# Paired 64-row gate matmuls, one attention block per pair of heads, and element-wise work on GpSimd in a two-layer hybrid step

## The chip, the core and the metric

The kernel runs on one core of a Trainium2 chip. A core has five engines with instruction queues of their own, each worked off in order: TensorE (PE, matrix products into PSUM banks), VectorE (DVE), ScalarE (ACT), GpSimd (POOL) and SyncE (SP, which here only issues DMAs). They wait for one another through semaphores. The metric is the device time of one execution in microseconds (us). The kernel before takes 1232.82 us, the median of three runs (1231.01 to 1233.5).

## What is computed

Two layers are applied to 128 context tokens and 256 latent tokens (384 columns here, features on the 128 partitions). Per layer, cut to what the change touches:

```
h = RMSNorm(x) * (1 + scale1) + shift1            # shift/scale/gate = SiLU(cond) @ w_mod + b_mod
u = h @ w_in                                      # u_pool, u_q, u_k, u_v, u_x, u_y, u_g (gates)
y_a = multi-scale pooling of u_pool, a 128x128 map per group
y_b = attention (context: dense; latent: neighbourhood + all context keys)
xc  = depthwise conv (width 4) of u_x
rg, ig = sigmoid(xc @ wa[block] + ba), sigmoid(xc @ wx[block] + bx)   # 2 directions, 8 blocks of 64 channels
h_t = a_t h_(t-1) + sqrt(1 - a_t^2) * ig_t * xc_t,  a = exp(c * rg * log_sigmoid(lambda))
y_c = (forward + backward h) * gelu(u_y)
merged = sum over the 3 branches of sigmoid(u_g) * (branch @ w_branch);  x += gate1 * (merged @ w_out)
x += gate2 * SwiGLU(...);  at the end a final RMSNorm
```

## The kernel before

**Matrix products.** A product is done in three passes to keep precision: weights and activations are each split into a high and a low part (`whi`/`wlo`, `hh`/`hl`, ...), and `mm3` (L342 to L344) multiplies high by high, high by low weight, low by high weight. A job of eight weight tiles is 24 matmuls of 384 columns; `in` jobs (a 1024x128 slice of w_in) have eight tiles, `br` jobs (w_branch) and `pw` (pooling map) four. Each weight tile is loaded by SP (`raw`), cast to `whi` by ACT (L305) and turned into `wlo` by DVE (L314), some jobs ahead, in the fixed order of `chunk_order()`.

**Order of work.** The code is a recording: every helper appends instructions to its engines' queues in program order, so what stands earlier in the code stands earlier in each queue. `job()` records a job's matmuls, then calls `tick()` (advances every open evacuation generator by one `yield`, and starts one of the waiting ones in `lazy`), `side_step()` (advances the side branches: the LRU scans and the attention), records its own evacuation, and calls `after(units)`. `after` adds `modr * units` to an accumulator `macc`, and for each whole unit records one `mod_step()`: half a row of SiLU(cond) @ w_mod, done on DVE as a product of a 128x1024 weight tile `wm` with `crow` (L262, output `junk`). `modr` is taken from the table `MR`, by layer and stage; its entry 6 holds for the five `in` jobs at the start of layer 0 (0.1 each there), entry 0 for the first stage of gate and branch jobs (`bi` = 0). The very first `mod_step()` calls `silu_crow()`: two tanh on ACT into `crt` (L233) and two updates of `crow` on DVE (L234). The tiles `crt` and `wm` share two buffers, so the load of the first `wm` (SP, L247) can't be issued before the first `crow` update has read its `crt`.

**A layer.** `in` jobs for the pool, x and y columns, with the pooling (`branch_pool`: `ws`, `pd`, split into `pdh`/`pdl`) and the convolution (`branch_conv`: `xp`, `cv`, split into `xch`/`xcl`) as evacuations; then `pool_proj` (four products of four groups: 12 matmuls, evacuated into `yah`, `yal`); then, for the branch order b = 0, 2, 1, eight pairs of a gate job (`win(24 + b*8 + d)`, evacuated by a tanh into `tg`) and a `br` job. During b = 0 the four `lru_gates(c)` stand at d = 2, 4, 6 and at the end; then the values job, the q/k jobs, b = 2 beside the attention, b = 1, and w_out. In layer 0 the pooling and convolution evacuations wait in `lazy`, since their inputs need a correction (`shw`, from the matmuls `mt`, L1168) that is computed at the end of `start()`, ahead of the five `in` jobs.

**Recurrent gates.** Each 64x64 block pair of wa and wx is stored as a block-diagonal 128x128 tile. `lru_gates(c)` does for each of the two directions two `mm3` of 386 columns over the full height, into two PSUM banks, and two tanh of 128 partitions (L616, L617).

**Attention.** 16 units (head pair p, query tile, head). A generator `branch_attn` does one step i per side step, in which the stages of the softmax of successive units are staggered: scores (64-row matmuls, both heads alternating, L702) at i, `soft_a` at i-1, `soft_b` at i-2, `soft_c` at i-3, transposes (full-height matmuls, L744) at i-4, their evacuation at i-5, values (64-column matmuls, L779) on every second step.

Of the kernel before, what the change touches and what calls it, by code (L numbers as in the profile page):

```python
# [90 lines left out]
def emit(ctx, tc, A, outs):  # L91
# [204 lines left out]
    def w_hi(n):  # L296
        while ws["cv"] < min(n, len(order)):
# [7 lines left out]
            S.activation(hi[:, :nk], r[:, :nk], AF.Copy)  # L305
# [298 lines left out]
    def lru_gates(l, c, w, y):  # L604
# [3 lines left out]
        for e in range(2):  # L608
            pa, px = psum(), psum()
            mm3(pa, w, (c % 2) * 4 + e * 2, mv, True, True, n=LW)  # L610
            mm3(px, w, (c % 2) * 4 + e * 2 + 1, mv, True, True, n=LW)

            def ev(pa, px, i, e):
# [13 lines left out]
                S.activation(t2[:, n], t2[:, n], AF.Identity, scale=-1.0, bias=1.0)  # L627
                y["lru", c, e] = (t2, th, ti)
            push(ev(pa, px, e * 4 + c, e))

    def branch_lru_scan(l, y):
# [13 lines left out]
        for c in range(4):  # L645
# [16 lines left out]
            V.tensor_tensor(yc[:, :NT], yc[:, :NT], hs[1][:, :NT], op=OP.add)  # L662
            V.tensor_tensor(yc[:, :NT], yc[:, :NT], y.pop(("gy", c))[:, :NT], op=OP.mult)
# [26 lines left out]

    def branch_attn(l, y):
# [90 lines left out]
        i = 0  # L782
        while i < nu + 7 or pend:
            if i < nu and ("k", units[i][0]) not in y:
                yield
# [4 lines left out]
            if 0 <= i - 1 < nu:  # L790
                p, hh, qt = units[i - 1]
                pr[i - 1] = soft_a(pr[i - 1], 2 * p + hh, qt)
            if 0 <= i - 2 < nu:
                soft_b(pr[i - 2])
            if 0 <= i - 3 < nu:
                soft_c(pr[i - 3])
# [81 lines left out]
    def ev_branch(th, bi, d, mg, mo):  # L878
        def f(ps):
# [55 lines left out]
    def start(y):  # L935
# [230 lines left out]
        ps = psum("mt")  # L1166
        for g in range(7):
            T.matmul(ps[:, 2 * g:2 * g + 2], sb[g // 3][:, (g % 3) * 128:(g % 3) * 128 + 128], sel,  # L1168
                     start=True, stop=True)
        shw = cp.tile([128, 14], F32, name="shw0")  # L1170
        V.tensor_copy(shw, ps[:, 0:14])
        evs = [ev_pool(0, g, y) for g in range(4)] + [ev_ux(0, c, y) for c in range(3)]
        for g, ev in enumerate(evs):
            lazy.append(ev((un[g], shw[:, 2 * g:2 * g + 2])))
# [137 lines left out]
def layout(i):  # L1312
# [37 lines left out]
    lru = np.zeros((L, 4, 2, 2, 128, 128), np.float32)  # L1350
    for w, name in enumerate(("lru_wa", "lru_wx")):
        a = f[name]
        for ch in range(4):
            for half in range(2):
                r = slice(64 * half, 64 * half + 64)
                lru[:, ch, :, w, r, r] = a[:, :, 2 * ch + half]
    A["lru"] = c(lru.reshape(L, 2, 8, 128, 128).transpose(0, 1, 3, 2, 4))
# [32 lines left out]
```

## Time and profile before

| what | value |
|---|---|
| median of 3 runs | 1232.82 us |
| profiled execution, its own time | 1231.6 us |
| its span (first to last instruction) | 1229.8 us |
| PE busy | 1219.8 us, 99% |
| DVE, ACT, POOL busy | 888.3 (72%), 598.4 (49%), 72.6 us (6%) |

The profile lists instructions with a start and a duration. A matmul's duration (0.33 us for 384 columns) overlaps its neighbour's: what one costs PE is the distance from its start to the next start. A group "x3" in a timeline is three like instructions in a row, from the first start to the last end. In brackets stands the idle time of the engine ahead of it and what ended that.

### The profile page before, as it was taken

Reading aid. Unit: us, or ns where it says so; the run is one execution under the profiler, and the core shown is the slowest. Engines: PE = TensorE matmul, PEld = TensorE weight load, DVE = VectorE, ACT = ScalarE, POOL = GpSimd, SP = SyncE. Lnnn points to the kernel's source line nnn. Section 1 sums busy time; section 2 is a strip of 40 time slices with the busy share of each in tenths; the row PEclk is TensorE's granted clock in tenths of the full one; section 3 lists DMA queues with packets and bytes.
Section 4 is the critical chain, followed back from the end, with each engine's and each line's share of the span. In section 5 each row is a group of like instructions: output and inputs, shape, how many; then the busy total and the mean of one; then the engine's idle time right before and its main releaser. Section 6 shows DMA issues by size and latency. Waiting matters only on the chain.

```text
span 1229.8 us, 19387 instructions
## 1 busy us (share of the span) xinstructions
PE 1219.8 (99%) x7348; PEld 1190.6 (97%) x7348; DVE 888.3 (72%) x1650; ACT 598.4 (49%) x1103; POOL 72.6 (6%) x187
## 2 busy tenths in 40 slices
PE   9999999999999999999999999999999999999997
PEld 7799999899999999999999999999999999999997
DVE  6798698998978887757779668787676785442432
ACT  5587845544455333333357576564344743332321
POOL 0000150000200000010000013100010000000000
PEclk9999999999999999999999999999999999999999
DMA  9635684466626666645643457632553355333321
GB/s 346 256 132 190 187 177 134 147 209 217 202 98 207 235 226 212 202 150 182 214 138 113 158 167 190 142 118 100 172 197 129 119 207 171 131 109 108 115 88 52
DMA packets 63645, 204.30 MB, mean 166 GB/s; under 512 B 7744, under 2 KB 10944, under 8 KB 63424
## 3 DMA queue, kind: packets, MB, share of 16 engines
q1 hardware_dynamic: 60912, 197.56, 48.2%
q0 software_dynamic: 2496, 5.25, 3.5%
q8 instruction: 57, 0.93, 0.3%
q14 instruction: 36, 0.29, 0.1%
q10 hardware_dynamic: 144, 0.26, 0.1%
HBM read 200.41 MB, written 2.63 MB: 165 GB/s over the span
## 4 chain that ended last, share of the span: by engine, by line
PE 58%; issue 22%; DVE 1%; POOL 0%; POOLq 0%; DVEq 0%
PE ps L342 18%; PE ps L344 18%; PE ps L343 18%; PE tp L744 1%; PE o L779 1%; PE sc L702 1%; PE vt L1210 0%; PE vt L1211 0%; PE vt L1212 0%; DVE junk L262 0%; DVE wlo L314 0%; PE o L774 0%; DVE pr L718 0%; PE st L473 0%; DVE yo L1306 0%
## 5 line engine op out<-in xcount | busy, mean ns | idle before, releaser
L342 PE MATMUL ps<-hh,whi 128*128 128x384 f32 x1256 | 422.2, 336 | 0.0
L344 PE MATMUL ps<-hl,whi 128*128 128x384 f32 x1256 | 419.9, 334 | 0.0
L343 PE MATMUL ps<-hh,wlo 128*128 128x384 f32 x1256 | 419.7, 334 | 0.0
L314 DVE TENSOR_TENSOR wlo<-raw,whi 128x1024 fp32r<-128x1024 f32 (+2 forms) x296 | 322.8, 1115 | 21.7 <-ACT whi L305 21.7
L305 ACT ACTIVATE whi<-raw 128x1024 fp32r<-128x1024 f32 (+2 forms) x296 | 279.8, 970 | 97.3 <-PE ps L344 59.8
L342 PEld LDWEIGHTS ps<-hh,whi 128*128 128x128 f32 x1256 | 235.7, 188 | 2.4 <-issue 0.3
L343 PEld LDWEIGHTS ps<-hh,wlo 128*128 128x128 f32 x1256 | 235.8, 188 | 0.1
L344 PEld LDWEIGHTS ps<-hl,whi 128*128 128x128 f32 x1256 | 235.7, 188 | 0.0
L262 DVE SCALAR_TENSOR_TENSOR junk<-wm,crow 128x1024 bf16<-128x1024 f32 x160 | 195.4, 1221 | 27.0 <-DMA wm<-in_wm 25.0
L909 ACT ACTIVATE ft<-ps 128x384 f32<-128x384 f32 x40 | 19.7, 493 | 202.8 <-PE ps L344 202.8
L342 PE MATMUL ps<-svh,whi 128*128 128x384 f32 x352 | 117.6, 334 | 0.0
L343 PE MATMUL ps<-svh,wlo 128*128 128x384 f32 x352 | 117.6, 334 | 0.0
L344 PE MATMUL ps<-svl,whi 128*128 128x384 f32 x352 | 117.6, 334 | 0.0
L894 DVE SCALAR_TENSOR_TENSOR x<-ps,modv,x 128x128 f32<-128x128 f32 x64 | 23.7, 412 | 81.6 <-PE ps L344 81.5
L911 DVE TENSOR_TENSOR ft<-ft,ps 128x384 f32<-128x384 f32 x40 | 22.1, 552 | 80.7 <-ACT ft L909 80.7
L872 ACT ACTIVATE tg<-ps 128x384 f32<-128x384 f32 x48 | 23.4, 489 | 89.0 <-PE ps L344 88.2
L342 PEld LDWEIGHTS ps<-svh,whi 128*128 128x128 f32 x352 | 66.1, 188 | 0.0
L343 PEld LDWEIGHTS ps<-svh,wlo 128*128 128x128 f32 x352 | 66.1, 188 | 0.0
L344 PEld LDWEIGHTS ps<-svl,whi 128*128 128x128 f32 x352 | 66.1, 188 | 0.0
L881 DVE SCALAR_TENSOR_TENSOR tg<-tg,ps 128x384 f32<-128x384 f32 x48 | 26.4, 551 | 44.0 <-PE ps L344 43.9
L453 ACT ACTIVATE sq<-x 128x384 f32<-128x384 f32 x40 | 20.1, 513 | 66.4 <-DVE x L894 66.4
L342 PE MATMUL ps<-mgh,whi 128*128 128x384 f32 x128 | 42.8, 334 | 0.0
(242 smaller groups left out, 1770.7 us busy)
## 6 DMA issues: line engine op xcount, KB each, us to landing
raw<-in_fi SPq DMA_DIRECT2D x88, 512.0 KB, 4.3
raw<-in_in SPq DMA_DIRECT2D x82, 512.0 KB, 3.9
wm<-in_wm SPq DMA_DIRECT2D x80, 512.0 KB, 4.3
raw<-in_fo SPq DMA_DIRECT2D x32, 512.0 KB, 4.6
raw<-in_br SPq DMA_DIRECT2D x48, 256.0 KB, 2.7
w<-in_wm SPq DMA_DIRECT2D x16, 512.0 KB, 7.0
raw<-in_wo SPq DMA_DIRECT2D x16, 512.0 KB, 3.7
raw<-in_fo SPq DMA_DIRECT2D x16, 384.0 KB, 3.1
```

The lines of the kernel that those rows point to most:

```text
L262: V.scalar_tensor_tensor(j, t, 0.5, crow[:, s], op0=OP.mult, op1=OP.mult, accum_out=modv[l][:, comp, d, s:s + 1])
L305: S.activation(hi[:, :nk], r[:, :nk], AF.Copy)
L314: V.tensor_tensor(lo[:, :nk], r[:, :nk], hi[:, :nk].bitcast(F32), op=OP.subtract)
L342: T.matmul(ps[:, :n], hi[:, k], mv[0][:, :n], start=start, stop=False)
L343: T.matmul(ps[:, :n], lo[:, k], mv[0][:, :n], start=False, stop=False)
L344: T.matmul(ps[:, :n], hi[:, k], mv[1][:, :n], start=False, stop=stop)
L453: S.activation(sq[:, :NT], xt[d], AF.Square)
L872: S.activation(t[:, :NT], ps[:, :NT], AF.Tanh, scale=0.5)
L881: V.scalar_tensor_tensor(t[:, :NT], t[:, :NT], 1.0, ps[:, :NT], op0=OP.add, op1=OP.mult)
L894: V.scalar_tensor_tensor(xt[d][:, o:o + n], ps[:, o:o + n], modv[l][:, comp, d, s:s + 1], xt[d][:, o:o + n], op0=OP.mult, op1=OP.add)
L909: S.activation(t[:, :NT], pg[:, :NT], AF.Silu)
L911: V.tensor_tensor(t[:, :NT], t[:, :NT], pu[:, :NT], op=OP.mult)
```

## The change

The recurrent gates are stored as 64x128 weights (wa for one half of the rows, wx for the other columns): `lru_gates` now records three pairs of matmuls per direction that use rows 0 to 63 and rows 64 to 127 into two banks, and evacuates with four tanh of 64 partitions. The four calls stand at d = 0, 2, 4, 6 in place of d = 2, 4, 6 and the end, so that the first follows `pool_proj` directly; `pool_proj`, with the emptying of `lazy` ahead of it, comes after the first gate job and not before it. In layer 0 the matmuls `mt` and what hangs on them (`rest()`) stand behind the first of the five `in` jobs. `MR` for layer 0 has 1.1 in place of 0.7 for the first stage, and 1.9, 1.6, 0.5 in place of 2.3, 1.8, 0.3 for the next three. The attention does transposes of two units, values and the next scores in one block on every second step. GpSimd takes the casts of the first branch's `br` weights and of the `vw` weights (from ACT), the affine step on `t2` (from ACT), the mask, the two steps on `yc` and the merge sums `mg` (from DVE); ACT takes the copy `ptc` from DVE. The diff, cut to its core:

```diff
-MR = ((0.7, 2.3, 1.8, 0.3, 1.3, 1.1, 0.1), (0.6, 0.8, 0.8, 0.3, 1.3, 0.7, 0))
+MR = ((1.1, 1.9, 1.6, 0.5, 1.3, 1.1, 0.1), (0.6, 0.8, 0.8, 0.3, 1.3, 0.7, 0))
...
-            S.activation(hi[:, :nk], r[:, :nk], AF.Copy)
+
+            if order[i][0] == "vw" or order[i][0] == "br" and order[i][2] < 8:
+                G.tensor_copy(hi[:, :nk], r[:, :nk])
+            else:
+                S.activation(hi[:, :nk], r[:, :nk], AF.Copy)
...
-            pa, px = psum(), psum()
-            mm3(pa, w, (c % 2) * 4 + e * 2, mv, True, True, n=LW)
-            mm3(px, w, (c % 2) * 4 + e * 2 + 1, mv, True, True, n=LW)
+            pb = [psum(), psum()]
+            j = (c % 2) * 2 + e
+            for wi, mi in ((0, 0), (1, 0), (0, 1)):
+                for b in range(2):
+                    r = slice(64 * b, 64 * b + 64)
+                    T.matmul(pb[b][:, :LW], w[wi][r, j], mv[mi][r, :LW], start=wi + mi == 0, stop=mi == 1)
...
-                S.activation(th[:, n], pa[:, n], AF.Tanh, scale=0.5, bias=q[:, i:i + 1])
-                S.activation(ti[:, n], px[:, n], AF.Tanh, scale=0.5, bias=q[:, 8 + i:9 + i])
+                for t, o, f in ((th, 0, 0), (ti, 8, 1)):
+                    for b in range(2):
+                        r, rs = slice(64 * b, 64 * b + 64), slice(64 * (b ^ f), 64 * (b ^ f) + 64)
+                        S.activation(t[r, n], pb[b][rs, n], AF.Tanh, scale=0.5, bias=q[r, o + i:o + i + 1])
...
-                S.activation(t2[:, n], t2[:, n], AF.Identity, scale=-1.0, bias=1.0)
+                G.tensor_scalar(t2[:, n], t2[:, n], -1.0, 1.0, op0=OP.mult, op1=OP.add)
...
-            V.tensor_tensor(yc[:, :NT], yc[:, :NT], hs[1][:, :NT], op=OP.add)
-            V.tensor_tensor(yc[:, :NT], yc[:, :NT], y.pop(("gy", c))[:, :NT], op=OP.mult)
+            G.tensor_tensor(yc[:, :NT], yc[:, :NT], hs[1][:, :NT], op=OP.add)
+            G.tensor_tensor(yc[:, :NT], yc[:, :NT], y.pop(("gy", c))[:, :NT], op=OP.mult)
...
-            V.tensor_tensor(t, t, cmask.unsqueeze(1).to_broadcast([128, 6, 64]), op=OP.add)
+            G.tensor_tensor(t, t, cmask.unsqueeze(1).to_broadcast([128, 6, 64]), op=OP.add)
...
-                V.tensor_copy(pc[:, :128], tp[:, 384:512])
+                S.activation(pc[:, :128], tp[:, 384:512], AF.Copy)
...
-            if 0 <= i - 5 < nu:
-                pr[i - 5] = evac(*pr[i - 5])
-            if i % 2 and 0 <= i - 7 < nu:
-                values((i - 7) // 2)
-            if 0 <= i - 4 < nu:
-                pr[i - 4] = transp(pr[i - 4])
-            if i % 2 == 0 and i < nu:
-                p, hh, qt = units[i]
-                if qt == 0:
-                    begin(p)
-                pr[i], pr[i + 1] = scores(p, qt)
+            if i % 2 == 0:
+                for u in (i - 6, i - 5):
+                    if 0 <= u < nu:
+                        pr[u] = evac(*pr[u])
+            else:
+                for u in (i - 5, i - 4):
+                    if 0 <= u < nu:
+                        pr[u] = transp(pr[u])
+                if 0 <= i - 7 < nu:
+                    values((i - 7) // 2)
+                if i + 1 < nu:
+                    p, hh, qt = units[i + 1]
+                    if qt == 0:
+                        begin(p)
+                    pr[i + 1], pr[i + 2] = scores(p, qt)
...
-            V.tensor_tensor(mg[d][:, :NT], mg[d][:, :NT], t[:, :NT], op=OP.add)
+            G.tensor_tensor(mg[d][:, :NT], mg[d][:, :NT], t[:, :NT], op=OP.add)
...
         for m in todo:
+            if m == 20 and l == 0:
+                rest()
...
-        while lazy:
-            tick()
-        tick()
-        pool_proj(l, y)
...
             win(24 + b * 8, ev_gate(th), units=0.67)
+            if b == 0:
+                while lazy:
+                    tick()
+                tick()
+                pool_proj(l, y)
             for d in range(8):
-                if b == 0 and d in (2, 6):
-                    lw = w_get("lru", l, d // 4)
-                if b == 0 and d in (2, 4, 6):
-                    lru_gates(l, d // 2 - 1, lw, y)
+                if b == 0 and d % 2 == 0:
+                    if d % 4 == 0:
+                        lw = w_get("lru", l, d // 4)
+                    lru_gates(l, d // 2, lw, y)
```

On DVE around the first `pool_proj` of layer 0 the queue stood like this before (`pdl` goes to `pool_proj`, `xcl` to the first recurrent gates, `crow` and `junk` belong to the first `mod_step`):

```order
L362 TENSOR_TENSOR pdl<-pd,pdh 128x384
L599 SCALAR_TENSOR_TENSOR cv<-xp,par,cv 128x386 x3
L362 TENSOR_TENSOR xcl<-cv,xch 128x386
L599 SCALAR_TENSOR_TENSOR cv<-xp,par,cv 128x386 x3
L314 TENSOR_TENSOR wlo<-raw,whi 128x1024
L314 TENSOR_TENSOR wlo<-raw,whi 128x512
L362 TENSOR_TENSOR xcl<-cv,xch 128x386
L364 SCALAR_TENSOR_TENSOR yal<-ps,par,yah 128x384 x4
L314 TENSOR_TENSOR wlo<-raw,whi 128x1024
L362 TENSOR_TENSOR xcl<-cv,xch 128x386
L234 SCALAR_TENSOR_TENSOR crow<-crt,crow 128x1024 x2
L262 SCALAR_TENSOR_TENSOR junk,modv_102<-wm,crow 128x1024
```

and after the change so:

```order
L583 SCALAR_TENSOR_TENSOR pd<-ws,up 128x128
L583 SCALAR_TENSOR_TENSOR pd<-ws,up 128x256
L235 SCALAR_TENSOR_TENSOR crow<-crt,crow 128x1024 x2
L263 SCALAR_TENSOR_TENSOR junk,modv_102<-wm,crow 128x1024
L367 TENSOR_TENSOR pdl<-pd,pdh 128x384
L604 SCALAR_TENSOR_TENSOR cv<-xp,par,cv 128x386 x3
L367 TENSOR_TENSOR pdl<-pd,pdh 128x384
L604 SCALAR_TENSOR_TENSOR cv<-xp,par,cv 128x386 x3
L367 TENSOR_TENSOR xcl<-cv,xch 128x386
L604 SCALAR_TENSOR_TENSOR cv<-xp,par,cv 128x386 x3
L319 TENSOR_TENSOR wlo<-raw,whi 128x1024
```

The two `crow` updates and the first `junk` stood behind `yal`, and now stand ahead of the last two `pdl` and of all three `cv` chains.

On PE at the same place (from the last but one group of `pool_proj`, `pdh`/`pdl`) the queue was before:

```order
L342 MATMUL ps<-pdh,whi 128x384
L343 MATMUL ps<-pdh,wlo 128x384
L344 MATMUL ps<-pdl,whi 128x384
L342 MATMUL ps<-pdh,whi 128x384
L343 MATMUL ps<-pdh,wlo 128x384
L344 MATMUL ps<-pdl,whi 128x384
L342 MATMUL ps<-hh,whi 128x384
L343 MATMUL ps<-hh,wlo 128x384
L344 MATMUL ps<-hl,whi 128x384
L342 MATMUL ps<-hh,whi 128x384
```

and is now:

```order
L349 MATMUL ps<-pdl,whi 128x384
L347 MATMUL ps<-pdh,whi 128x384
L348 MATMUL ps<-pdh,wlo 128x384
L349 MATMUL ps<-pdl,whi 128x384
L620 MATMUL ps<-xch,whi 128x386 x2
L620 MATMUL ps<-xch,wlo 128x386 x2
L620 MATMUL ps<-xcl,whi 128x386 x2
L620 MATMUL ps<-xch,whi 128x386 x2
L620 MATMUL ps<-xch,wlo 128x386 x2
L620 MATMUL ps<-xcl,whi 128x386 x2
L347 MATMUL ps<-hh,whi 128x384
L348 MATMUL ps<-hh,wlo 128x384
```

The gate job (`hh`, `hl`) followed `pool_proj` directly; now the first recurrent gates, in six pairs of 64-row matmuls, stand between them.

On PE within the attention (`tp` transposes, `o` values, `sc` scores) one of the places before was:

```order
L744 MATMUL tp<-ident,pr 128x128 x3
L744 MATMUL tp<-ident,pc 128x128
L702 MATMUL sc<-k,q 128x256 x2
L702 MATMUL sc<-ckv,q 128x128 x2
L702 MATMUL sc<-k,q 128x128 x2
```

and one of those after is:

```order
L757 MATMUL tp<-ident,pr 128x128 x6
L787 MATMUL o<-ptc,vv 64x128 x2
L792 MATMUL o<-pt,vv 64x128 x4
L792 MATMUL o<-pt,ckv 64x128 x2
L715 MATMUL sc<-k,q 128x256 x2
L715 MATMUL sc<-ckv,q 128x128 x2
L715 MATMUL sc<-k,q 128x128 x2
```

Transposes of one unit and the scores stood together, and the values elsewhere with another unit's transposes; now the transposes of two units, the values and the scores of a pair stand in one place.

## Rows read from the trace of the kernel before

**Rows 1.** Page: the span, and PE's busy time.

```profile
span 1229.8 us, 19387 instructions
...
PE 1219.8 (99%) x7348; PEld 1190.6 (97%) x7348; DVE 888.3 (72%) x1650; ACT 598.4 (49%) x1103; POOL 72.6 (6%) x187
```

**Rows 2.** Waits of PE: waited for, total us, times, longest.

```profile
PE mt L1168 <- ACT mb L1165: 1.0, 1, 1.0
PE tp L744 <- DVE pr L735: 0.6, 1, 0.6
```

**Rows 3.** Timeline, PE: one call of the recurrent gates; columns start us, duration us.

```profile
97.84 0.34 PE L342 MATMUL ps<-xch,whi 128*128 128x386 f32 x1
...
99.95 0.34 PE L342 MATMUL ps<-hh,whi 128*128 128x384 f32 x1
```

**Rows 4.** Timeline, PE, in the attention.

```profile
225.67 0.49 PE L744 MATMUL tp<-ident,pr 128*128 128x128 f32 x3
225.99 0.27 PE L744 MATMUL tp<-ident,pc 128*128 128x128 f32 x1
226.20 0.70 PE L702 MATMUL sc<-k,q 64*128 64x256 f32 x4
226.73 0.39 PE L702 MATMUL sc<-ckv,q 64*128 64x128 f32 x4
226.95 0.39 PE L702 MATMUL sc<-k,q 64*128 64x128 f32 x4
227.27 0.44 PE L342 MATMUL ps<-hh,whi 128*128 128x384 f32 x1
227.55 0.33 PE L343 MATMUL ps<-hh,wlo 128*128 128x384 f32 x1
...
231.39 0.34 PE L344 MATMUL ps<-hl,whi 128*128 128x384 f32 x1
231.66 0.66 PE L779 MATMUL o<-pt,vv 128*64 128x128 f32 x8
```

**Rows 5.** Timeline, DVE, about the first pool_proj of layer 0.

```profile
78.38 2.00 DVE L599 SCALAR_TENSOR_TENSOR cv<-xp,par,cv 128x386 f32<-128x386 f32 x3 [0.82 <-ACT cv L596]
80.30 0.55 DVE L362 TENSOR_TENSOR pdl<-pd,pdh 128x384 fp32r<-128x384 f32 x1
...
91.81 2.35 DVE L234 SCALAR_TENSOR_TENSOR crow<-crt,crow 128x1024 f32<-128x1024 f32 x2
96.71 1.23 DVE L262 SCALAR_TENSOR_TENSOR junk<-wm,crow 128x1024 bf16<-128x1024 f32 x1 [2.54 <-DMA wm<-in_wm]
```

**Rows 6.** Timeline, ACT, the same place.

```profile
84.58 1.98 ACT L359 ACTIVATE yah<-ps,par 128x384 fp32r<-128x384 f32 x4
...
89.72 0.49 ACT L872 ACTIVATE tg<-ps 128x384 f32<-128x384 f32 x1 [0.46 <-PE ps L344]
90.11 2.00 ACT L233 ACTIVATE crt<-crow 128x1024 f32<-128x1024 f32 x2
...
98.56 0.58 ACT L616 ACTIVATE th<-ps,dpall 128x386 f32<-128x386 f32 x1 [1.59 <-PE ps L344]
```

**Rows 7.** Windows: length, busy us by engine (instructions), granted PE clock, DMA.

```profile
81.00:139.60 58.60, 58.60 (x338) 58.60 (x338) 47.68 (x72) 44.68 (x74) 2.67 (x4) 1.00 0.56 176
203.50:264.20 60.70, 60.10 (x438) 55.12 (x437) 58.01 (x145) 32.70 (x84) 0.00 (x0) 1.00 0.48 154
1223.30:1228.00 4.70, 0.02 (x1) 0.00 (x0) 1.75 (x3) 1.52 (x3) 0.00 (x0) 1.00 0.77 296
1228.00:1229.80 1.80, 0.00 (x0) 0.00 (x0) 0.00 (x0) 0.00 (x0) 0.00 (x0) 0.55 0.26 100
```

**Rows 8.** Timeline, PE: first matmuls of the kernel.

```profile
1.36 3.78 PE L1050 MATMUL warm<-ident 128*128 128x128 f32 x16 [1.36 <-POOL ident masks.py:199]
```

**Rows 9.** Timeline, POOL, two sums of 128x2.

```profile
327.82 0.19 POOL L448 TENSOR_TENSOR xsl<-modv,xsh 128x2 fp32r<-128x2 f32 x1
...
328.23 1.31 POOL L448 TENSOR_TENSOR xsl<-modv,xsh 128x2 fp32r<-128x2 f32 x1
```

More of the change, by code (lines that the diff above doesn't have):

```diff
@@ L58, in chunk_order @@
         o += [("in", l, m, 8) for m in ms]
-        o += [("pw", l, 0, 4)]
         for b in (0, 2, 1):
             o += [("in", l, 24 + b * 8, 8)]
+            if b == 0:
+                o += [("pw", l, 0, 4)]
             for d in range(8):
-                if b == 0 and d in (2, 6):
-                    o += [("lru", l, d // 4, 8)]
+                if b == 0 and d in (0, 4):
+                    o += [("lru", l, d // 4, 4)]
                 if d < 7:
@@ L780, in values @@
                              start=jj == 0, stop=jj == 2, skip_group_check=True)
-        i = 0
+        i = -1
         while i < nu + 7 or pend:
-            if i < nu and ("k", units[i][0]) not in y:
+            if i % 2 and i + 1 < nu and ("k", units[i + 1][0]) not in y:
                 yield
@@ L789, in branch_attn @@
                     pend.remove(g)
+            if 0 <= i < nu:
+                p, hh, qt = units[i]
+                pr[i] = soft_a(pr[i], 2 * p + hh, qt)
             if 0 <= i - 1 < nu:
[L791 to L792 removed]
+                soft_b(pr[i - 1])
             if 0 <= i - 2 < nu:
[L794 to L807 removed]
+                soft_c(pr[i - 2])
+            if i % 2 == 0:
[13 more added lines that the diff above has]
+                    pr[i + 1], pr[i + 2] = scores(p, qt)
             if i % 4 == 2 and 0 <= i - 10 < nu:
@@ L1165, in start, with rest @@
             S.activation(sb[hf][:, :n], fb[hf][:, :n], AF.Copy)
[L1166 to L1174, printed above, removed]
+        def rest():
+            ps = psum("mt")
+            for g in range(7):
+                T.matmul(ps[:, 2 * g:2 * g + 2], sb[g // 3][:, (g % 3) * 128:(g % 3) * 128 + 128], sel,
+                         start=True, stop=True)
+            shw = cp.tile([128, 14], F32, name="shw0")
+            V.tensor_copy(shw, ps[:, 0:14])
+            evs = [ev_pool(0, g, y) for g in range(4)] + [ev_ux(0, c, y) for c in range(3)]
+            for g, ev in enumerate(evs):
+                lazy.append(ev((un[g], shw[:, 2 * g:2 * g + 2])))
         load_crow()
         w_ahead(0)
-        return mv
+        return mv, rest
     for l in range(L):
@@ L1181, in emit @@
         if l == 0:
-            mv = start(y)
+            mv, rest = start(y)
             todo = [19, 20, 21, 22, 23]
@@ L1233, in emit @@
             win(24 + b * 8, ev_gate(th), units=0.67)
-            for d in range(8):
-                if b == 0 and d in (2, 6):
-                    lw = w_get("lru", l, d // 4)
-                if b == 0 and d in (2, 4, 6):
-                    lru_gates(l, d // 2 - 1, lw, y)
+            if b == 0:
+                while lazy:
+                    tick()
+                tick()
+                pool_proj(l, y)
+            for d in range(8):
+                if b == 0 and d % 2 == 0:
+                    if d % 4 == 0:
+                        lw = w_get("lru", l, d // 4)
+                    lru_gates(l, d // 2, lw, y)
+                    if d % 4 == 2:
+                        lw = None
                 if d < 7:
@@ L1353, in layout @@
         for ch in range(4):
[L1354 to L1357, printed above, removed]
+            for b in range(2):
+                o = 64 * (b ^ w)
+                lru[:, ch, :, 64 * b:64 * b + 64, o:o + 64] = a[:, :, 2 * ch + b]
+    A["lru"] = c(lru.reshape(L, 2, 4, 128, 128).transpose(0, 1, 3, 2, 4))
     br = f["w_branch"].reshape(L, 3, 4, 128, 8, 128).transpose(0, 1, 4, 3, 2, 5)
```

9 lines of the change are left out of this document (4 added, 5 removed).

## The prediction

> **What bounds the kernel now.** I read the page's busy times first, to see which engine has no slack: PE works 1219.8 of a span of 1229.8 us [rows 1]. Second the waits of PE, which name only two of interest: 1.0 us for the statistics correction `mb` at the start, and 0.6 us once in the attention, for `pr` from DVE [rows 2]. So PE sets the end nearly everywhere. A change gains only what it takes from PE's queue, its mode changes or these two waits; work moved between DVE, ACT and GpSimd gains nothing by itself; and a new wait of PE is lost in full. Third I read the timelines of PE, DVE and ACT where the change moves instructions, and last the windows, for how near the other engines stand to their limit: DVE has 47.7 of 58.6 us in the first gate stage of layer 0 but 58.0 of 60.7 beside the attention [rows 7].
>
> **What is taken from PE.** (1) Recurrent gates. A call of 12 full-height matmuls takes from 97.84 to 99.95, 2.11 us, or 0.176 us each [rows 3]. There are eight calls (four in each of two layers), 96 matmuls, 16.9 us. The change has as many matmuls, but of 64 rows, in pairs into two banks. The trace has no such pair at 386 columns; it has pairs of 64-row matmuls in the scores, where four of 128 columns start from 226.73 to 226.95, 0.055 us each, while full-height transposes of the same 128 columns start from 225.67 to 225.99 for three, 0.107 us each [rows 4]. So a pair runs in the time of one, and 48 pair times of 0.176 us come to 8.5 us in place of 16.9: 8.5 us saved (16.9 less 48 x 0.176, rounded), with 0 as the other bound if the pairs run one after the other. I take 8.5, since the scores are the same form. A change of mode has a price. Into 64 rows: the four transposes take 4 x 0.107 from 225.67, which is 226.10, and the scores start at 226.20, 0.10 late. Out of it: the last four scores should be done at 226.95 + 0.22 = 227.17, the next job starts at 227.27, and its second matmul comes 0.28 later in place of 0.17 [rows 4]: 0.10 + 0.11. With as much again inside the first scores (four of 256 columns take 226.20 to 226.73, 0.53 against 4 x 0.11) an excursion is 0.4 us. Eight excursions: 3.2 us. Net gain 5.3.
>
> (2) Attention. Values also cost a change: from 231.39 the next start would be 0.17 later but comes after 0.27 [rows 4], and the same again behind, 0.3 in all. Eight score and eight value blocks per layer cost 8 x (0.4 + 0.3) = 5.6 us. Now values and scores of a pair stand together: four breaks with scores alone at 0.4, four with both at 0.55, four with values alone at 0.35, 5.2 in all. Two layers: 0.9 gained (bounds 0 to 2). The wait of 0.6 on `pr` goes too, since `soft_c` is now two steps ahead of the transposes instead of one.
>
> (3) Start. With `mt` behind an `in` job, the wait of 1.0 for `mb` [rows 2] is covered by 4.2 us of matmuls. Gains: 5.3 + 0.9 + 0.6 + 1.0 = 7.8 us.
>
> **What is added to PE's path.** (4) The first recurrent gates of layer 0. The accumulator of `after` holds 0.5 after five `in` jobs; the first gate job adds 0.67 x 0.7 = 0.47 before (0.97, nothing yet), and 0.67 x 1.1 = 0.74 now (1.24). So the first `mod_step`, with `silu_crow`, is recorded in that job, and DVE's queue has both `crow` and the first `junk` ahead of the last two `pdl` and the `cv` chains, as the order of the two programs shows. Before, PE was through `pool_proj` when this chain ran, and nothing waited. Now `pool_proj` and `xcl` stand behind it. Let T be the end of the first gate job. ACT does `tg` and starts the first `crt` 0.39 later, of 1.0 us each (89.72, 90.11, two in 2.00) [rows 6]: the first `crow` can start at T + 1.45. From the start of the first `crow` to the start of `junk` it took 91.81 to 96.71, 4.90 us, the last 2.54 of it idle for the DMA of `wm`, whose buffer the first `crow` frees [rows 5]; nothing in the change shortens this. `junk` starts at T + 6.35, takes 1.23: T + 7.6. Then `pdl` 0.5: T + 8.1; three `cv` 1.92 (78.38 to 80.30): T + 10.0; `pdl`: T + 10.5; three `cv`: T + 12.4; `xcl` 0.55: T + 13.0 [rows 5]. PE can then finish the first direction (T + 13.5), and the next gate job can start only when a bank is free again. All eight are taken by `pool_proj` and these gates, and the first to come free is read by the third half-tanh: three of 0.58 with their overlap [rows 6] are 1.6, T + 15.1. Unhindered PE would be there at T + 3.5 (twelve `pool_proj` matmuls at 0.173, six pairs at 0.176, 0.4 for the mode). Loss 11.6 us, with bounds 10 and 13.5 as the transfer comes 0.7 sooner or the pooling chain ahead of `crow` ends up to 1.5 us after T.
>
> (5) Layer 1 has no such step there, but the same banks: the four `yah` (1.98 for four [rows 6]) end some 0.6 after `pool_proj`, two half-tanh of `th` and one of `ti` follow the first direction's end at about 1.1, so the bank is free at 2.6 when PE is done at 1.5: loss 1.1 (bounds 0 and 2).
>
> (6) The clock. PE idles from T + 1.4 (eight matmuls of `pool_proj` done) to T + 8.1. At the end of the kernel PE stands from 1223.3, the granted clock is 1.00 to 1228.0 and 0.55 after [rows 7]: it fell about 4.7 us after the last matmul, from 2.4 to 1.2 GHz. So it may fall here too. At the lower level the first 16 matmuls of the kernel take 3.78 us, 0.23 each, where 128 columns later take 0.107 [rows 4, 8]. If some 4 to 5 us of work run so, 2.2 are lost; I count 1.5 (bounds 0 and 3). The Trainium skill, "TensorE: Matmul & The Clock Gate", Part 1, says that the clock is withdrawn from an idle PE and given back only after sustained work; the rows above agree, and no run yet shows it in the middle of this kernel.
>
> (7) GpSimd. Its sums in the merge lie before w_out with little room; I count 0.3. The casts for `br` and `vw`, the masks, `yc` and `t2` are made some jobs ahead, and ACT, with 44.7 of 58.6 us busy [rows 7], takes 32 half-tanh more and gives up as many casts and copies: 0. If that cover is gone, the price is rival C.
>
> **Sum.** 1231.6 - 7.8 + 11.6 + 1.1 + 1.5 + 0.3 = 1238.3 us for the profiled execution (span 1229.8 and 1.8 around it), 6.7 us more. It lies 1.2 under the median of 1232.8, so for a median I say 1239.5.
>
> **Rivals.** A: The stall of (4) is hardly there, since `crow` and `junk` don't hold the chain. Without the stretch from T + 1.45 to T + 7.6 the bank comes free at T + 9, a loss of 5.4; if DVE has also worked ahead during the gate job, only the wait of (5) is left, 1.1. The middle is 3.3, and 1231.6 - 7.8 + 3.3 + 1.1 + 0.3 = 1228.5, or 1229.7 as a median: faster. For it speaks that PE comes to `pool_proj` one job later than before; against it that DVE works its queue in order and that `junk` can't start before its DMA has landed, which the row shows as idle time. It decides if `junk` starts less than about 2 us after T.
>
> B: The 64-row pairs don't run together at 386 columns of this type. Then 8.5 is not saved: 1248. Against it stand the scores' rows.
>
> C: DVE and GpSimd hold each other up. A GpSimd sum of 128x2 took 0.19 us once and 1.31 us soon after [rows 9], when DVE had a `wlo` in work, an operation with two inputs from SBUF. A merge sum is like `pdl` on DVE, 0.55 us [rows 5]. Beside the attention DVE has 2.7 us to spare in 60.7 [rows 7]; it gives up some 22 sums and masks (12 us), and if each of these takes between 0.55 and 1.1 us on GpSimd and shuts DVE out, DVE's time is between 58 and 70, so up to 9 us are lost in layer 0, half that as a middle: 1244. In layer 1 there is room. The Trainium skill, "SBUF — State Buffer", Who interferes with whom, says that a DVE instruction with two SBUF inputs and a GpSimd instruction that reads SBUF exclude each other for the whole of an instruction, whoever starts first; "GPSIMD Engine Reference", 4.1, puts two-input work there at about twice VectorE's time, an estimate of 1.1 us for a merge sum. By both the sum would be rival C's upper half. The row shows GpSimd waiting for DVE, none shows DVE waiting for GpSimd, and so I give it less than the forecast.
>
> **Chances.** Forecast 0.52, A 0.20, B 0.10, C 0.13, other 0.05. What a measurement here can tell from no change is about 0.2%, 2.5 us: below 1230.4 is faster, above 1235.3 slower. Of the forecast's 0.52, 0.46 is slower and 0.06 the same (stall at 10, clock kept, gains at their upper bounds); A gives 0.14 faster and 0.06 the same; B, C and the rest give 0.24 slower, 0.03 the same and 0.01 faster. Together 0.15, 0.15 and 0.70. The forecast's own range is 1235 to 1244. The range that takes in most of A's and C's cases, and B's lower half, is 1230 to 1248.
>
> **What would show it.** In the profile after: one wait of PE of 6 to 7 us at the third group of `pool_proj` on DVE `pdl`, about 82 us, then 2 us and 2.5 us more on `pdl` and `xcl`, then 1 to 1.5 us of the next gate job on ACT; `junk` idle for DMA ahead of it; the granted clock below 1 right there; six pairs at 0.176 us and eight calls at some 1.5 us; no wait for `mb` and `pr`. It is wrong if the waits about 82 us sum to less than 8, if a call of the gates takes 2 us or more, or if PE waits for `whi` or `wlo` beside the attention.

## The result, and the profile after

The changed kernel takes 1242.4 us (median of four runs, 1241.81 to 1243.23), the kernel before in the same comparison 1233.1. The ratio is 1.0074, 95% interval 1.0062 to 1.0085: slower by 9.3 us. The forecast was 1239.5. In the profiled executions the span grew from 1229.8 [rows 1] to 1240.4 us, while PE's busy time fell a little. From the page of the changed kernel:

```profile
span 1240.4 us, 19525 instructions
...
PE 1218.9 (98%) x7348; PEld 1186.7 (96%) x7348; DVE 896.3 (72%) x1570; ACT 597.0 (48%) x1111; POOL 204.1 (16%) x291
```

So the loss is waiting: the time in which PE is idle grew from 10.0 to 21.5 us (span less busy time), while PE's busy time hardly changed, though the paired gates take less of it; most of what they save, slower matmuls take (below). The waits of PE in the changed kernel (waited for, total us, times, longest):

```profile
PE ps L349 <- DVE pdl L367: 7.8, 2, 6.8
PE ps L347 <- ACT ti L629: 3.3, 2, 2.0
...
PE o L787 <- ACT ptc L766: 1.2, 1, 1.2
PE ps L620 <- DVE xcl L367: 0.8, 1, 0.8
```

The two waits of before for `mb` and `pr` [rows 2] are gone; new are 7.8 us for `pdl`, 0.8 for `xcl`, 3.3 for the half-tanh `ti` (2.0 in layer 0, 1.4 in layer 1) and 1.2 for `ptc`. PE's timeline after the first gate job shows the first three in one place (start us, us, idle before in brackets):

```profile
90.10 0.69 PE L349 MATMUL ps<-pdl,whi 128*128 128x384 f32 x1 [6.79 <-DVE pdl L367]
...
92.48 0.69 PE L349 MATMUL ps<-pdl,whi 128*128 128x384 f32 x1 [1.05 <-DVE pdl L367]
...
94.87 0.69 PE L620 MATMUL ps<-xcl,whi 64*128 64x386 f32 x2 [0.76 <-DVE xcl L367]
...
98.50 0.69 PE L347 MATMUL ps<-hh,whi 128*128 128x384 f32 x1 [1.97 <-ACT ti L629]
```

The first gate job ends at 81.75 (T), and the next starts at 98.50: T + 16.75, where 3.5 would do by the prediction's count. DVE in the same stretch:

```profile
83.42 2.36 DVE L235 SCALAR_TENSOR_TENSOR crow<-crt,crow 128x1024 f32<-128x1024 f32 x2 [5.65 <-ACT crt L234]
88.34 1.23 DVE L263 SCALAR_TENSOR_TENSOR junk<-wm,crow 128x1024 bf16<-128x1024 f32 x1 [2.55 <-DMA wm<-in_wm]
...
89.49 0.55 DVE L367 TENSOR_TENSOR pdl<-pd,pdh 128x384 fp32r<-128x384 f32 x1
...
94.26 0.56 DVE L367 TENSOR_TENSOR xcl<-cv,xch 128x386 fp32r<-128x386 f32 x1
```

DVE idles for 5.65 us for `crt`, does `crow`, idles for 2.55 us for the transfer of `wm`, and only then comes to `pdl`: from the first `crow` to `junk` it is 4.92 us, as the 4.90 of before [rows 5]. ACT:

```profile
81.95 0.49 ACT L890 ACTIVATE tg<-ps 128x384 f32<-128x384 f32 x1 [0.82 <-PE ps L349]
82.34 1.99 ACT L234 ACTIVATE crt<-crow 128x1024 f32<-128x1024 f32 x2
...
94.81 1.98 ACT L364 ACTIVATE yah<-ps,par 128x384 fp32r<-128x384 f32 x4
96.66 1.18 ACT L629 ACTIVATE th<-ps,dpall 64x386 f32<-64x386 f32 x2
97.86 1.18 ACT L629 ACTIVATE ti<-ps,dpall 64x386 f32<-64x386 f32 x2
```

`crt` starts 0.39 after `tg` as before [rows 6]. The half-tanh stand behind the four `yah`, and two of them take 1.18. Windows of the stretch (start and end, length, busy time of PE, PEld, DVE, ACT, POOL with instructions, then the granted clock, DMA share, GB/s):

```profile
83.50:88.00 4.50, 0.00 (x0) 0.00 (x0) 2.29 (x2) 2.64 (x5) 0.00 (x0) 0.94 0.41 137
88.00:98.50 10.50, 4.62 (x17) 2.76 (x17) 9.74 (x17) 5.98 (x13) 0.00 (x0) 0.50 0.11 42
98.50:104.40 5.90, 5.90 (x18) 5.90 (x19) 2.54 (x5) 5.74 (x9) 0.00 (x0) 0.50 0.40 133
```

Between 4 and 5 us after PE's last matmul the granted clock fell to half, 1.2 GHz, and it stayed there through the first 18 matmuls of the next gate job, which start 0.32 us apart (98.50 to 104.40) where 0.17 is usual.

The whole span can be set out by the starts of PE's stages in the two timelines. Up to T the changed kernel is 1.4 us ahead (0.3 of it already ahead of the first instruction that the change moves); from T to the values job of layer 0 it loses 13.3 (13.25 in the stall, 2.7 by the clock, less 2.6 for four calls of paired gates); the attention of layer 0 loses 0.3; layer 1 gains 1.2 up to its values and 0.6 in its attention. Together 10.6, the difference of the spans.

### The profile page after: what moved, and what is told of

Read it like the earlier page. It is cut to its first block, busy times and chain, and to the rows that moved or that the text cites. A ratio compares the mean times of both kernels' runs of the same rounds, so it can differ in the third digit from the quotient of the medians.

```text
span 1240.4 us, 19525 instructions
## 1 busy us (share of the span) xinstructions
PE 1218.9 (98%) x7348; PEld 1186.7 (96%) x7348; DVE 896.3 (72%) x1570; ACT 597.0 (48%) x1111; POOL 204.1 (16%) x291
## 4 chain that ended last, share of the span: by engine, by line
PE 59%; issue 22%; DVE 1%; ACT 0%; POOLq 0%; POOL 0%; DVEq 0%
PE ps L347 18%; PE ps L348 18%; PE ps L349 18%; PE o L792 1%; PE sc L715 1%; PE tp L757 1%; PE vt L1233 0%; PE vt L1234 0%; PE vt L1232 0%; PE ps L620 0%; DVE wlo L319 0%; PE o L787 0%; DVE junk L263 0%; PE st L478 0%; DVE pr L731 0%
## 5 line engine op out<-in xcount | busy, mean ns | idle before, releaser
L319 DVE TENSOR_TENSOR wlo<-raw,whi 128x1024 fp32r<-128x1024 f32 (+2 forms) x296 | 338.3, 1168 | 46.9 <-ACT whi L310 44.9
L310 ACT ACTIVATE whi<-raw 128x1024 fp32r<-128x1024 f32 (+2 forms) x272 | 259.9, 981 | 85.4 <-PE ps L349 56.5
L263 DVE SCALAR_TENSOR_TENSOR junk<-wm,crow 128x1024 bf16<-128x1024 f32 x160 | 204.2, 1276 | 24.1 <-DMA wm<-in_wm 22.4
L903 POOL TENSOR_TENSOR tg<-tg 128x384 f32<-128x384 f32 x32 | 57.3, 1792 | 171.7 <-DVE tg L899 171.7
L488 POOL TENSOR_TENSOR rs<-ms,mhalf 128x3 f32<-128x3 f32 x5 | 4.4, 873 | 368.6 <-DVE ms L484 270.8
```

The costliest lines, as they stand in the source:

```text
L263: V.scalar_tensor_tensor(j, t, 0.5, crow[:, s], op0=OP.mult, op1=OP.mult, accum_out=modv[l][:, comp, d, s:s + 1])
L319: V.tensor_tensor(lo[:, :nk], r[:, :nk], hi[:, :nk].bitcast(F32), op=OP.subtract)
L903: G.tensor_tensor(mg[d][:, :NT], mg[d][:, :NT], t[:, :NT], op=OP.add)
```

## The experiments

All were run beside the kernel before; the ratio is to it, with its 95% interval. Theory 1: the order on DVE (`crow` and `junk` ahead of `pdl` and `xcl`) makes the stall, and the stall makes the clock fall. Rivals: the recurrent gates directly behind `pool_proj`, with all eight banks taken; exclusion between GpSimd and DVE.

**MR of before in the changed kernel.**

```diff
-MR = ((1.1, 1.9, 1.6, 0.5, 1.3, 1.1, 0.1), ...
+MR = ((0.7, 2.3, 1.8, 0.3, 1.3, 1.1, 0.1), ...
```

> The changed kernel with the table MR of before, so that the first mod_step (crow, junk) stands behind the yal operations on DVE and not ahead of pool_proj. Theory 1 (the queue order of crow and junk on DVE makes the stall of 13 us about 82 us, and the stall makes the clock fall, 2.9 us): PE waits about 82 to 92 us for 5 us in all in place of 13.3 and the granted clock stays at 1.00, so 1242.4 - 8.2 - 2.9 = 1231.3 us (1229.5 to 1233). Rival 2 (the recurrent gates directly behind pool_proj are the cause, since pool_proj and the gates take all eight banks): the time stays above 1239. Rival 3 (GpSimd and DVE hold each other up): above 1239 too.

Measured 1234.6 us, ratio 1.0015 (1.0006 to 1.0025): 7.8 of the 9.3 us are back, from one row of the table. It is 3 us above the expectation. Its waits of PE:

```profile
PE ps L347 <- ACT ti L629: 3.9, 2, 2.6
PE ps L347 <- DVE ybl L367: 1.7, 1, 1.7
PE ps L620 <- DVE xcl L367: 1.5, 1, 1.5
...
PE ps L348 <- DVE wlo L319: 1.0, 1, 1.0
PE ps L620 <- ACT xch L364: 0.5, 1, 0.5
```

Of the stall, `pdl` is gone, but `xcl` 1.5, `ti` 2.6, `xch` 0.5 and `wlo` 1.0 us are left in layer 0, and the clock is at 0.50 from 88 to 93 us here as well. Theory 1 holds for the larger part; a second part is there.

**`crow` early, all else as changed.**

```diff
-        if mst["run"] == 0:
+        if mst["run"] == 0 and not mst.get("silu"):
             silu_crow()
...
             if m == 20 and l == 0:
                 rest()
+            if m == 22 and l == 0:
+                mst["silu"] = True
+                silu_crow()
+                mod_dma(2)
```

> The changed kernel with its own MR, but with the two crow updates and the first two wm loads recorded after the fourth of the five in jobs, so that junk finds its wm landed. The order of everything else stays, junk too stands ahead of pdl. Theory 1: the wait for crow, and junk's wait for the transfer, were what PE stood for; 1231.3 us as with MR of before, at most 1.2 more for junk. If instead DVE's mere work (junk, pdl, six cv) between the first gate job and xcl were the cause, 1238 or more.

Measured 1237.5, ratio 1.0037 (1.0025 to 1.0050), 4.9 less than the changed kernel, 6 above the expectation and just under the 1238 of its alternative, that DVE's mere work is the cause. `junk` now has its data, but the two `crow` updates stand on DVE ahead of the pooling, and `xcl` comes at 89.13 where with MR of before it comes at 86.33:

```profile
83.22 1.22 DVE L263 SCALAR_TENSOR_TENSOR junk<-wm,crow 128x1024 bf16<-128x1024 f32 x1
...
89.13 0.55 DVE L367 TENSOR_TENSOR xcl<-cv,xch 128x386 fp32r<-128x386 f32 x1
```

So the waits on DVE, of `crow` for `crt` and of `junk` for the transfer, were some 5 us of the loss (with what they cost in clock); the mere DVE work in front (`crow` 2.4, `junk` 1.2) was 3 more.

**Filler on PE during the stall.**

```diff
+            pdv = y.pop(("pd", g))
+            if l == 0 and g == 2:
+                for _ in range(38):
+                    T.matmul(ps[:, :NT], w[0][:, g], pdv[0][:, :NT], start=True, stop=True)
...
```

> The changed kernel with 38 more matmuls of 384 columns (6.6 us) on PE ahead of the third group of pool_proj in layer 0, whose sums are overwritten by the group itself; they run while PE waits for pdl. Theory 1: the wait is the same, but the clock doesn't fall, and the matmuls from 98.5 to 104.5 us run at 174 instead of 320 ns: 2.9 us less, 1239.5 us (1239 to 1240.5). If the clock costs nothing of its own: 1242.4.

Measured 1242.3, ratio 1.0072 (1.0057 to 1.0087): no gain, against the expectation. The filler ran to 89.4 us and the clock stayed at 1.00 through it, but it fell all the same, behind the two waits of 1.6 us (`pdl`) and 1.4 us (`xcl`) that follow, and was low through the third, of 2.0 us (`ti`):

```profile
92.00:96.00 4.00, 2.29 (x13) 1.63 (x13) 3.72 (x8) 3.54 (x8) 0.00 (x0) 0.84 0.00 0
96.00:98.00 2.00, 0.36 (x4) 0.00 (x0) 2.00 (x3) 1.95 (x5) 0.00 (x0) 0.50 0.00 0
```

The price of the clock by itself is thus not shown by a run; the 2.7 us are read from the changed kernel's timeline.

**The 64-row pairs alone, at the places of before.**

```diff
-            mm3(pa, w, (c % 2) * 4 + e * 2, mv, True, True, n=LW)
-            mm3(px, w, (c % 2) * 4 + e * 2 + 1, mv, True, True, n=LW)
...
+            for wi, mi in ((0, 0), (1, 0), (0, 1)):
+                for b in range(2):
+                    T.matmul(pb[b][:, :LW], w[wi][r, j], mv[mi][r, :LW], ...)
```

> The kernel before with the 64-row pairs alone (weights, six pairs per call, four half-tanh), at the places of before, t2 on ACT. All theories: eight calls at 0.66 us less each, 1233.1 - 5.3 = 1227.8 us (1227 to 1229). If pairs only gain while others are idle, or the half-tanh hold PE up at the end of the stage: 1230 or more.

Measured 1238.6, ratio 1.0041 (1.0026 to 1.0056): slower than before by 5.5 us, the wrong side of the expectation. The gate stages are 2.8 us shorter each, near the 2.6 that was forecast; all of it and more goes later:

```profile
PE sc L709 <- ACT k L856: 4.1, 2, 3.2
PE tp L751 <- DVE pr L742: 2.6, 2, 2.0
```

PE stands 3.2 us for `k` in layer 0. On ACT the chain from the last call of the gates to `k` is later. In the kernel before (its `ych` started at 164.83):

```profile
165.26 0.47 ACT L849 ACTIVATE k<-ps 128x384 f32<-128x384 f32 x1
```

and with the pairs:

```profile
168.48 0.52 ACT L359 ACTIVATE ych<-hf 128x384 fp32r<-128x384 f32 x1 [2.10 <-DVE hf L670]
168.91 0.47 ACT L856 ACTIVATE k<-ps 128x384 f32<-128x384 f32 x1
```

Four half-tanh of 0.59 per direction take the place of two of 0.57, and the last call stands at the end of the stage; the eight roots, the scans on DVE, `ych` and, behind it in ACT's queue, `k` all move back by 3.65 us, while PE comes sooner. The waits are not the whole of it: behind the one for `k` the granted clock is 0.50 from 170 to 174 us, and behind the 2.0 us for `pr` in layer 1 it is 0.57 from 790 to 794 us; by the starts of PE's stages this takes some 3 us in layer 0's attention and 2 in layer 1's.

**The attention alone.** The edit is the hunk of the change on `i = -1 ...`, in the kernel before.

> The kernel before with the attention in one block per pair alone (ptc by ACT left out: DVE copies it). By the prediction's terms 0.9 of mode changes and the wait of 0.6 for pr go: 1233.1 - 1.5 = 1231.6 us. If the later evacuation (two units together) puts a wait for pt or ptc on PE, as the changed kernel has one of 1.2 us, 1232.8 or more.

Measured 1233.4, ratio 1.0002 (0.9993 to 1.0011): no change. The wait for `pr` is gone, and one of 1.6 us takes its place:

```profile
PE ps L342 <- DVE ybl L362: 1.6, 1, 1.6
```

**GpSimd alone.** The hunks `S.`/`V.` to `G.` (casts, `t2`, mask, `yc`, merge sums), in the kernel before.

> The kernel before with the work on GpSimd alone: casts of the first br and the vw weights, the affine step on t2, mask, both yc steps, merge sums (ptc stays on DVE). Forecast: PE never waits for these, 1233.1 us within 1.5. Rival C (exclusion between GpSimd and DVE): the merge sums take 1.8 us and the yc steps 1.0 to 1.9, and those on the chain from the scans to the first scores delay PE: 1236 to 1240, with waits of PE for k (ACT behind ych) as in the run of the 64-row pairs alone.

Measured 1240.5, ratio 1.0051 (1.0036 to 1.0066): rival C's price, 6.3 us by the ratio and 7.4 by the medians. The profiled execution shows one wait that has grown from 0.6 [rows 2] to 4.3 us, in the attention, not at `k`:

```profile
PE tp L748 <- DVE pr L739: 4.3, 2, 3.5
```

The larger of the two waits, 3.5 us, lies at 784 us. Here are, from the same execution, GpSimd's two steps on `yc` (`hf`), ACT, DVE, and a window with the columns as above:

```profile
781.48 2.05 POOL L666 TENSOR_TENSOR hf<-hf 128x384 f32<-128x384 f32 x1
783.61 1.86 POOL L667 TENSOR_TENSOR hf<-hf,gy 128x384 f32<-128x384 f32 x1
...
785.50 0.52 ACT L363 ACTIVATE ych<-hf 128x384 fp32r<-128x384 f32 x1 [4.22 <-POOL hf L667]
...
786.22 0.29 DVE L719 TENSOR_REDUCE m<-sc 128x1 f32<-128x128 f32 x1 [1.60 <-ACT pr L714]
...
790.00:794.00 4.00, 4.00 (x20) 3.72 (x17) 3.90 (x9) 1.77 (x6) 0.95 (x2) 0.56 0.40 137
```

In the kernel before, DVE did these two steps in 0.55 and 0.56 us at 778.33 and 778.91. On GpSimd they start at 781.48, behind DMA issues in its queue, and take 2.05 and 1.86 us, and DVE's `wlo` beside them takes 2.02 where one of this size took 1.22 shortly before. ACT stands 4.22 us for them with `ych`; ACT's `pr`, next in its queue, is late by that, and so are DVE's softmax and PE's transposes. Behind the wait the clock is low: the matmuls from 788.02 to 793.66 take 5.64 us, the same ones 3.11 in the kernel before. Wait and clock, 3.5 and 2.5 us, are the loss of this execution but for some 0.6 us in layer 0's attention.

**All but the places and MR.** The changed kernel with `pool_proj`, the gates and MR where they were before.

```diff
-                if b == 0 and d % 2 == 0:
+                if b == 0 and d in (2, 4, 6):
...
+                lru_gates(l, 3, lw, y)
```

> The changed kernel with pool_proj ahead of the first gate job and the recurrent gates at d = 2, 4, 6 and the end, as before, and the MR of before; pairs, attention, GpSimd work and the late mt stay. Theory 1a (the run of the pairs alone lost its gain because the last call of the gates stands at the end of the stage: eight half-tanh on ACT in place of four, then roots, scans and ych ahead of k): PE waits for k by 2 to 4 us in layer 0, the time is 1227 to 1232. If the places don't matter: 1233.1 - 5.3 - 1.4 - 1.5 = 1224.9.

Measured 1237.7, ratio 1.0031 (1.0021 to 1.0041). The wait for `k` is only 0.6, but the values job behind the last gates waits for the last `tg` of DVE:

```profile
PE vt L1231 <- DVE tg L898: 3.8, 2, 2.6
...
PE ps L348 <- DVE pdl L366: 1.5, 1, 1.5
...
PE ps L346 <- ACT pdh L363: 0.9, 1, 0.9
```

And with the late `mt`, `pool_proj` at its old place finds `pdh` and `pdl` not ready (2.4 us).

**The same with the gates at d = 1, 3, 4, 6.**

```diff
-                if b == 0 and d in (2, 4, 6):
+                if b == 0 and d in (1, 3, 4, 6):
...
```

> As the one with the places of before, but the recurrent gates at d = 1, 3, 4, 6, so that a pair of jobs lies between pool_proj and the first call, and the last call is one pair of jobs and more before the end. Theory 1a: no wait about 82 us, none for k, all gains stand: 1224 to 1227 us. If it is at 1230 or more, something else of the change costs time.

Measured 1232.3, ratio 0.9985 (0.9975 to 0.9994). With the gates earlier the wait of the values job is gone (5.4 us less than the run before); the 2.4 at `pool_proj` and `ybl` 1.7 stay, and 0.6 for `ptc` is new. The time is 5 us above the expectation, and "No wait about 82 us" was wrong.

**Changed kernel, MR of before, gates at d = 1, 3, 4, 6.**

```diff
-                if b == 0 and d % 2 == 0:
+                if b == 0 and d in (1, 3, 4, 6):
...
```

> The changed kernel with the MR of before and the recurrent gates at d = 1, 3, 4, 6 in place of 0, 2, 4, 6; pool_proj stays behind the first gate job. Theory 1: with crow out of the way, what is left of the stall in the run with MR of before (xcl 1.5, ti 2.6, xch 0.5, wlo 1.0 us, and the clock) comes from the first gates standing directly behind pool_proj; with a gate and a branch job between it is gone, PE waits for nothing before 130 us, the clock stays at 1.00: 1234.6 - 5.6 - 1.5 = 1227.5 us (1226 to 1229). If it is above 1231, the rest of the stall has another cause.

Measured 1232.9, ratio 0.9998 (0.9989 to 1.0007), 1.7 less than with the gates at d = 0, and 5 above the expectation. The rest of the stall did not go, it changed its name:

```profile
PE ps L349 <- DVE yal L369: 3.2, 1, 3.2
```

The first branch job needs `yal`, which stands on DVE behind `cv`, `wlo` and `xcl`. So the second part of the loss isn't the banks of the gates alone. The reading is that with `mt`, and so the pooling, 2.9 us later, ACT and DVE are behind PE here, and whoever reads from them first waits. The two runs before show it at `pool_proj` (2.4 us at its old place), but no run has the late `mt` by itself, so this is argued and not shown. The rival of the gates behind `pool_proj` is worth the 1.7 us of this run at most.

**Pairs, late `mt`, `pool_proj` behind the first gate, gates at d = 1, 3, 4, 6; attention and GpSimd as before.** The edits are those above, without the hunks of the attention (with `ptc` on ACT) and of `G.`; one more `yield`, which the change has ahead of DVE's steps in the evacuation of the gates, is left out too.

> The kernel before with the 64-row pairs, the late mt, pool_proj behind the first gate job and the gates at d = 1, 3, 4, 6, but the attention of before and nothing on GpSimd. Theory: the gains that no run has contradicted stand (5.3 for the pairs, 1.3 for the start), none of the losses of the attention (ybl, 1.7) and of GpSimd: 1226.5 us (1225 to 1228). If ACT, with 32 half-tanh more and without relief by GpSimd, holds up the first scores as in the run of the pairs alone, 1229 to 1234.

Measured 1229.9, ratio 0.9973 (0.9963 to 0.9984): faster than before, 3.1 less than the run with GpSimd and the attention, and still with 2.9 us for `yal`.

**The new MR alone, in the kernel before.** The edit is the one line of MR.

> The kernel before with the new MR alone. There pool_proj stands ahead of the first gate job, so crow and junk come behind pdl and xcl in any case. Theory 1 (it is the place of the two together): no wait of PE about 82 us, 1233.1 us within 1.5. If the new table costs by itself: 1238 or more.

Measured 1232.1, ratio 0.9991 (0.9982 to 1.0000): the table costs nothing where `pool_proj` stands ahead of the first gate job. It costs 7.8 us in the changed order.

**The pairs alone with the gates at d = 1, 3, 4, 6.** The edits are those of the pairs and of the places, in the kernel before.

> The kernel before with the 64-row pairs alone, as in the run of the pairs at the places of before, but with the four calls at d = 1, 3, 4, 6 in place of 2, 4, 6 and the end; mt, pool_proj, MR, attention and GpSimd as before. If the loss of that run came from the last call at the end of the stage (ACT's half-tanh, then roots, scans, ych ahead of k), the gain of 5.3 stands in full: 1233.1 - 5.3 = 1227.8 us (1226.5 to 1229). If ACT's 32 half-tanh more cost by themselves, PE still waits for k: 1231 or more.

Measured 1228.3 (1227.8 to 1230.7), ratio 0.9962 (0.9948 to 0.9975): the full gain of the pairs, and the fastest version, 14 us below the changed kernel. Its waits of PE are those of before:

```profile
PE mt L1175 <- ACT mb L1172: 1.0, 1, 1.0
PE tp L751 <- DVE pr L742: 0.6, 1, 0.6
```

The run with pairs, late `mt` and `pool_proj` behind the first gate differs from this one by those two places, and takes 1229.9: against the forecast of a gain of 1.0, they bring none there (the intervals of the two ratios overlap).

## Why the prediction was right

The mechanism was right in its place and in its steps. T was 81.75; `crow` began at T + 1.67 (1.45 forecast), `junk` at T + 6.59 (6.35), the `pdl` of the third group was read at T + 8.35 (8.1), `xcl` at T + 13.1 (13.0). The waits forecast as 6 to 7, 2, 2.5 and 1 to 1.5 us were 6.8, 1.05, 0.76 and 1.97 (together 10.6, where less than 8 would have spoken against it), with matmuls at the slow clock between them: DVE sets the distance from one to the next, so what the slow clock adds to the matmuls there only shortens the waits.

Three terms were too small. The next gate job began at T + 16.75, not 15.1: the half-tanh started at T + 14.9 and not 13.5, because the four `yah` stand ahead of them in ACT's queue, which step (5) counted and the sum of step (4) left out, and they take 0.60 from start to start, not 0.53. The clock cost 2.7 (18 matmuls at 0.32 in place of 0.17), not 1.5. Its price had been read from the first 16 matmuls of the kernel as if at the lower level, but the profile of before grants 1.00 from 0 to 6 us, so that row doesn't show it; the 0.32 does. The wait of 1.2 for `ptc` wasn't foreseen: two units are evacuated together, and the second `pt`, which by the program takes a buffer that DVE's softmax reads last, starts only at 218.82; with the attention alone, where DVE copies `ptc`, there is none. With 1.65, 1.2 and 1.2 more, 1238.3 becomes 1242.3; the profiled execution took 1242.2. That it comes out so closely is partly luck, since smaller misses cancel: the start is 0.4 further ahead, the wait of step (5) was 1.4 and not 1.1, and the 0.3 of term (7) is seen nowhere. In term (2), two layers at 5.6 less 5.2 are 0.8, not 0.9.

The gains: a call of the gates in the middle of the stage shows the pairs as forecast.

```profile
113.71 0.34 PE L349 MATMUL ps<-yal,whi 128*128 128x384 f32 x1
113.97 0.45 PE L620 MATMUL ps<-xch,whi 64*128 64x386 f32 x2
...
115.23 0.45 PE L347 MATMUL ps<-hh,whi 128*128 128x384 f32 x1
115.51 0.34 PE L348 MATMUL ps<-hh,wlo 128*128 128x384 f32 x1
```

From 113.97 to 115.23 it takes 1.26 us, where 2.11 were [rows 3], with 0.09 more ahead and 0.10 behind: 0.66 saved, eight times 5.3. At T the start is 1.4 ahead, 0.3 of it from before any edit, so some 1.1 gained for 1.0. The attention gained 0.6 in layer 1 and lost 0.3 in layer 0; by the run with it alone its 1.5 us are nothing, since the waits for `ybl` or `ptc` eat them. What the prediction hadn't seen is that the pairs' gain hangs on the places of the calls: at the old ones it turns into a loss of 5.5, by ACT and not by PE as in rival B, which is refuted.

Rival A is refuted for the change as it stands: `junk` did not start within 2 us of T. With MR of before, where `crow` and `junk` don't hold the chain, 5.6 us of waits are left in layer 0 and some clock, more than its 3.3. Rival C was not the cause of the 9.3 us: the waits of the changed kernel name GpSimd nowhere, and one row of MR takes most of them away. But its mechanism is real; in the order of before the work on GpSimd alone costs 6.3 to 7.4 us, where term (7) had 0.3. In the changed order GpSimd and the attention (and the one `yield`) together cost 3.1 between two runs, of which `ybl` is 1.7, so 1 to 2 us of it can't be excluded. A merge sum takes 1.8 us on GpSimd, where the prediction took 0.55 for one on DVE (0.56 in the trace of before) and 1.1 at most on GpSimd:

```profile
L903 POOL TENSOR_TENSOR tg<-tg 128x384 f32<-128x384 f32 x32 | 57.3, 1792 | 171.7 <-DVE tg L899 171.7
```

## What to carry to other kernels

Before a job is moved ahead of another, write down what stands ahead of its inputs in the other engines' queues: a product whose data could be ready may stand behind an instruction that waits for a DMA. Where PE is busy for 99%, a cheaper product is worth its time only if the chain that starts from it (here half-tanh, roots, scans, `ych`, `k`) doesn't end later; the same pairs made the kernel 5.5 us slower at the old places and 5 us faster one or two pairs of jobs sooner. Run edits alone: of the four run so, two were neutral and two slower, and the one row that was neutral alone cost 7.8 us in company.

## What was not expected of the hardware

DVE's busy time rose from 888.3 [rows 1] to 896.3 us, although it has 80 instructions fewer: beside GpSimd its own take longer. Against the median of its group, no DVE instruction of the kernel before is longer by more than 0.15 us; in the changed kernel 69 are, by 48 us together, and in the run with GpSimd alone 71, by 48, every one of them while GpSimd is at work. In the runs without the new work on GpSimd (the pairs, the attention, the two with earlier gates) there is none. A `wlo` of 128x1024 takes 1282 ns in the mean where it was 1220. The group in the kernel before:

```profile
L314 DVE TENSOR_TENSOR wlo<-raw,whi 128x1024 fp32r<-128x1024 f32 x230 | 274.9, 1220 | 20.1 <-ACT whi L305 20.1
```

and after:

```profile
L319 DVE TENSOR_TENSOR wlo<-raw,whi 128x1024 fp32r<-128x1024 f32 x226 | 284.0, 1282 | 43.6 <-ACT whi L310 43.5
```

The Trainium skill, "SBUF — State Buffer", Who interferes with whom, says that a DVE instruction with two SBUF inputs and a GpSimd instruction that reads SBUF exclude each other; the means on both engines agree with it. One place shows an instruction of DVE held until GpSimd is done, GpSimd's two masks and DVE's step on the maxima `m`, which takes 0.17 us at 214.63:

```profile
209.28 1.96 POOL L702 TENSOR_TENSOR bias<-bias,cmask 128x384 f32<-128x384 f32 x2
...
209.48 1.80 DVE L735 TENSOR_SCALAR m<-m 128x2 f32<-128x2 f32 x1
```

The clock fell after waits much shorter than the one predicted from: in the run with later gates PE waited 3.2 us from 88.9, and the clock was at 0.50 from 92 to 96 us. And kernels with the wait of 1.0 us for `mb` show a lower clock there in some executions and not in others: in the profiled one of before it was 1.00 from 55 to 65 us, in that of the new MR alone 0.90 and 0.76,

```profile
55.00:60.00 5.00, 3.98 (x32) 3.83 (x25) 4.62 (x11) 5.00 (x10) 0.46 (x9) 0.90 0.31 105
60.00:65.00 5.00, 5.00 (x24) 5.00 (x24) 4.93 (x8) 2.79 (x7) 0.00 (x0) 0.76 0.88 258
```

and its `in` jobs took 1.6 us longer. The executions of before differ likewise: those with a mean granted clock of 0.999 take 1231.5 us in the median, those with 0.998 1233.2. So spans of single executions differ by as much as an edit here is worth, and only the medians and intervals decide between such kernels.
